# Attention of a hybrid trunk: probabilities stationary against both parts of v, a fixed softmax order, the residual loaded again, and GpSimd work moved

## The chip, the cores and the metric

The kernel runs on one core of one Trainium2 chip. The metric is the device time of one execution in microseconds, as the median of several runs. The profile shows one more execution of the same program: TensorE (PE, with its weight loads as PEld), VectorE (DVE), ScalarE (ACT), GpSimd (POOL) and SyncE's DMA queue (SP).

## The reference

One sequence of 512 tokens and 1024 features goes through four residual layers: attention, MLP, S5 state-space layer, MLP. The change lies in the first layer and in what is made for the third beside the first MLP. The attention is:

```python
c_q, c_kv, k_r, q_b, k_b, v_b = jnp.split(h @ w_in, IN_SPLITS, axis=-1)
q = (rms_norm(c_q, g_cq) @ w_uq).reshape(B, S, MLA_HEADS, MLA_QK).transpose(0, 2, 1, 3)
kv = (rms_norm(c_kv, g_ckv) @ w_ukv).reshape(B, S, MLA_HEADS, MLA_NOPE + MLA_V).transpose(0, 2, 1, 3)
...
s = jnp.einsum('bhqd,bhkd->bhqk', q[:, :, lo:hi], k[:, :, :hi]).astype(jnp.float32)
mask = jnp.arange(hi)[None, :] <= jnp.arange(lo, hi)[:, None]
p = jax.nn.softmax(jnp.where(mask, s, -jnp.inf), axis=-1).astype(v.dtype)
outs.append(jnp.einsum('bhqk,bhkd->bhqd', p, v[:, :, :hi]))
...
return o @ w_o
```

There are 8 latent heads (key width 96) and 8 MoBA heads (key width 64), values 64 wide. With 512 tokens in blocks of 256, a MoBA query's chosen past block and its own block are all the keys before it, so both kinds are causal attention over 512 tokens. The layer's output is added to x. The S5 layer is a convolution whose tables come from its parameters alone.

## The kernel before, in words

Every large product is made in three matmuls: an operand is split into a rounded part and the rest ("hi" and "lo", of type fp32r), and hi·hi, hi·lo and lo·hi are added in PSUM (`mm3`, L116 to L120). A weight tile is loaded by SP's queue (L109 or L155), its hi part is a copy on ACT (L112, L171), its lo part a subtraction on DVE (L113) or on the engine that is passed in (L172).

**Front** (`split_x`, L329 to L341, and `proj`, L343 to L366). For each of 8 slices of x: hi part on ACT (L331), lo part on DVE (L332), the square on POOL for even slices (L334, L340) and on ACT for odd ones (L338), the running sum of squares on POOL (L341); then the slice of w_in is split (L358 ACT, L359 DVE), and 12 matmuls follow (L362 to L364).

**The attention loop** (L622 to L644) takes 16 heads (8, 9, then 0 to 7, then 10 to 15) of 4 query blocks each, 64 steps (h, b), in a pipeline: in step i, block i+1 is transposed (stage c), block i+2 gets its exponentials (stage b), block i+3 its scores (stage a), and block i its product with v (stage d). Stage a makes the scores by three matmuls and a mask matmul (L522 to L525) and the row maxima on DVE (L527). Stage b is the exponential on ACT with its row sum (L535), the reciprocal on DVE (L536), and the scaling of the row by it (L537: ACT for odd b, DVE for even). Stage c transposes each 128 keys on PE (L545), copies the hi part on ACT (L548) and subtracts the lo part on DVE (L549). Stage d holds 64 columns of v stationary and streams 128 queries, three matmuls for each 128 keys (L564 to L566); after a head's last block its 64 x 512 output is split (L570 ACT, L571 DVE). The order of instructions on an engine is a scheduler's, which may move them past one another.

Between the steps stands filler work for PE, taken from lists (`segs`, L615) at an even rate: projections of MoBA pairs 1 to 3 from step -3 to 37, and the first half of the output projection w_o from step 42 to 62. The latter (`w_o1_items`) splits its weights with `gp`, POOL, as the engine of the lo part (L587, L172), and adds the residual in two steps, hi part and product on DVE (L599), lo part on POOL (L600). The tile xT of the residual, a buffer with one copy, held x and then the values v of heads 0 to 7.

**The S5 tables** (generator L890 to L994) are made during the first MLP. `pump` (L1387) advances the generator after each group of matmuls, and `behind` keeps a step's instructions after DVE's and POOL's last ones. Unit u of 16 makes W and its companion on POOL (L899, L901) and CP on DVE (L905, L907), rotates on POOL (L936 to L938) with a copy on ACT (L939) and a store (L940), places B (L946, L947), splits tables (L915 to L923), and multiplies them on PE (L955 to L957). W, CP and RT have two buffers each.

Of the kernel before, what the change touches and what calls it, by code (L numbers as in the profile page):

```python
# [45 lines left out]
class Trunk:  # L46
# [130 lines left out]
    def attention(self, xt, w_in, gmix, g_cq, w_uq, g_ckv, w_ukv, gains, rope, w_o, mlp):  # L177
# [24 lines left out]
        def moba_pair_items(p):  # L202
# [20 lines left out]
            def start():  # L223
                d["qk"] = mo.tile([P, NT, 4, 64], F32, name="qk", bufs=3)
                d["vh"] = mo.tile([P, NT, 2, 64], F32R, name="vh", bufs=3)
                d["vl"] = mo.tile([P, NT, 2, 64], F32R, name="vl", bufs=3)
                d["ss"] = mo.tile([P, NT, 4], F32, name="mss")
                d["r"] = mo.tile([P, NT, 4], F32, name="mr")
                self.pairs[p] = d["qk"], d["vh"], d["vl"]

            def unit(t, q):
# [9 lines left out]
                if q == 3:  # L241
# [3 lines left out]
                    vt = d["vh"][:, t].rearrange("p a d -> p (a d)")  # L245
                    sc.activation(vt, ps[:, 256:], AF.Copy, scale=rt)
                    ve.scalar_tensor_tensor(d["vl"][:, t].rearrange("p a d -> p (a d)"), ps[:, 256:], rt,
                                            f32(d["vh"])[:, t].rearrange("p a d -> p (a d)"),
                                            op0=OP.mult, op1=OP.subtract)
# [46 lines left out]
        with tc.tile_pool(name="att_e", bufs=1) as ep:  # L296
# [16 lines left out]
            for h in range(2):  # L313
# [10 lines left out]
            a = mo.tile([P, 1024], F32R, name="qk", bufs=3)  # L324
            cTs = [[a[:, j * 384:(j + 1) * 384].rearrange("p (c q) -> p c q", c=3) for j in range(2)],
                   [mo.tile([P, NT, 2, 64], F32R, name=v, bufs=3).rearrange("p t a d -> p (t a d)")
                    [:, :384].rearrange("p (c q) -> p c q", c=3) for v in ("vh", "vl")]]

            def split_x(k):  # L329
# [156 lines left out]
        O1 = [[op.tile([P, S], F32R, name=f"o1{2 * p + a}") for a in range(2)] for p in range(4)]  # L486
        O2 = [[op.tile([P, S], F32R, name=f"o2{a}") for a in "hl"]]
# [26 lines left out]
        st = {}  # L514

        def stage_a(h, b):
# [5 lines left out]
            pe.matmul(s[:, :n], q[0][rows, bs], k[0][rows, :n], start=True, stop=False)  # L522
# [3 lines left out]
            m = hd.tile([P, 4], F32, name="st", bufs=6)  # L526
            ve.reduce_max(m[:, 0:1], s[:, :n], axis=AX.X, negate=True)  # L527
            st[h, b] = dict(s=s, m=m)

        def stage_b(h, b):  # L530
# [4 lines left out]
            sc.activation(p[:, :n], d["s"][:, :n], AF.Exp, bias=m[:, 0:1], accum_out=m[:, 1:2])  # L535
            ve.reciprocal(m[:, 2:3], m[:, 1:2])  # L536
            sc.activation(p[:, :n], p[:, :n], AF.Copy, scale=m[:, 2:3]) if b % 2 else ve.tensor_scalar(p[:, :n], p[:, :n], m[:, 2:3], None, op0=OP.mult)  # L537

        def stage_c(h, b):
# [3 lines left out]
            for j in range(b + 1):  # L543
                js = slice(j * P, (j + 1) * P)
                pe.transpose(pt[:, js], d["p"][:, js], self.ident)  # L545
            ph = d["ph"] = hd.tile([P, 512], F32R, name="ph")
            pl = d["pl"] = hd.tile([P, 512], F32R, name="pl")
            sc.copy(ph[:, :n], pt[:, :n])  # L548
            ve.tensor_sub(pl[:, :n], pt[:, :n], f32(ph)[:, :n])  # L549

        def stage_d(h, b):
# [3 lines left out]
            po = st[h]  # L555
            if h < 8:
                v = vm_hi[:, :, h], vm_lo[:, :, h]
            else:
                _, vh, vl = self.pairs[(h - 8) // 2]
                v = vh[:, :, h % 2], vl[:, :, h % 2]  # L560
            bs = slice(b * P, (b + 1) * P)
            for j in range(b + 1):
                js = slice(j * P, (j + 1) * P)
                pe.matmul(po[:64, bs], v[0][:, j], d["ph"][:, js], start=j == 0, stop=False)  # L564
                pe.matmul(po[:64, bs], v[0][:, j], d["pl"][:, js], start=False, stop=False)
                pe.matmul(po[:64, bs], v[1][:, j], d["ph"][:, js], start=False, stop=j == b)  # L566
# [960 lines left out]
```

## Time and profile before

| | us |
|---|---|
| time, median of 3 runs | 1217.16 (1216.47 to 1218.07) |
| time of the profiled execution | 1217.28 |
| span from the first to the last instruction in it | 1215.5 |
| PE busy | 1155.7 (95%), 6296 matmuls |
| DVE busy | 788.6 (65%) |
| ACT busy | 501.2 (41%) |
| POOL busy | 257.9 (21%) |
| mean granted TensorE clock | 0.973 of full speed |

PE is busy nearly everywhere, so the stretches in which it is not, or in which its clock is below full speed, are what one reads first. The page cuts the span into 40 equal slices of 30.4 us (counted here from 0). PE's busy share is 7 tenths in slice 0, the front; 8 tenths in slice 2, where the attention loop begins, and in slices 14 and 16, from about 425 us; and 7 to 8 tenths in slices 22 to 24, the S5 layer itself, whose code the change leaves. The clock is at 7 to 8 tenths in slices 6 and 7, about 182 to 243 us, in slice 15, and in slices 22 to 24. The front lies at 0 to 32 us, the attention loop at about 62 to 276, the first MLP with the S5 tables at about 300 to 560.

### The profile page before, as it was taken

How to read it: one execution, taken by the hardware profiler on the slowest of the kernel's cores; microseconds unless marked ns; L12 is line 12 of the kernel's file. 1: busy time of each engine (PE TensorE's matmuls, PEld its weight loads, DVE VectorE, ACT ScalarE, POOL GpSimd, SP SyncE). 2: the span in 40 equal slices, each digit the busy share in tenths (PEclk: the TensorE clock that was granted, in tenths of full speed). 3: DMA queues.
4: the chain of work that ended last, by engine and by line, in shares of the span. 5: the costliest groups of instructions: out<-in, count | busy, mean ns of one | idle time of the engine just before them, and what ended most of it. 6: DMA issues, size and time to landing. Idle time of an engine off the chain costs nothing.

```text
span 1215.5 us, 16433 instructions
## 1 busy us (share of the span) xinstructions
PE 1155.7 (95%) x6296; PEld 963.5 (79%) x6296; DVE 788.6 (65%) x1381; ACT 501.2 (41%) x928; POOL 257.9 (21%) x260
## 2 busy tenths in 40 slices
PE   7989999999999989899999788999999999999998
PEld 6978997777888867788888576878788888888887
DVE  8887766668679979998855576553454444444444
ACT  5857775545331333352352265343341331322221
POOL 5461022224000588652300031111000000000000
PEclk9999997899999998999999788999999999999999
DMA  7302201114422357777769789522322332322421
GB/s 223 103 3 53 70 2 70 36 36 154 140 79 95 104 189 237 223 217 216 227 212 339 229 284 323 178 94 80 104 104 70 104 105 70 113 95 70 139 87 52
DMA packets 123758, 161.94 MB, mean 133 GB/s; under 512 B 15648, under 2 KB 72352, under 8 KB 120992
## 3 DMA queue, kind: packets, MB, share of 16 engines
q1 hardware_dynamic: 123680, 160.90, 40.8%
q8 instruction: 49, 0.80, 0.3%
q14 instruction: 29, 0.24, 0.1%
HBM read 133.75 MB, written 35.52 MB: 139 GB/s over the span
## 4 chain that ended last, share of the span: by engine, by line
PE 75%; DVE 9%; DMA 5%; POOL 4%; ACT 4%; issue 2%; SPq 1%; ACTq 0%; DVEq 0%; POOLq 0%
PE mm L118 14%; PE mm L120 14%; PE mm L119 14%; PE s L120 5%; PE s L118 5%; PE s L119 5%; DVE wlo L113 2%; PE pt L545 1%; PE mm L238 1%; PE mm L239 1%; PE mm L240 1%; DMA dX<-xT 1%; PE s L522 1%; PE pt L493 1%; POOL RT L938 1%
## 5 line engine op out<-in xcount | busy, mean ns | idle before, releaser
L112 ACT CAST whi<-wraw 128x1024 fp32r<-128x1024 f32 x132 | 131.8, 1048 | 229.7 <-PE mm L119 136.3
L113 DVE TENSOR_TENSOR wlo<-wraw,whi 128x1024 fp32r<-128x1024 f32 x132 | 168.7, 1307 | 77.4 <-ACT whi L112 77.3
L118 PE MATMUL mm<-ahi,whi 128*128 128x512 f32 (+1 forms) x352 | 135.8, 388 | 2.4 <-ACT ahi L1417 2.4
L119 PE MATMUL mm<-alo,whi 128*128 128x512 f32 (+1 forms) x352 | 136.3, 389 | 1.3 <-DVE alo L1418 1.3
L118 PE MATMUL mm<-xhi,whi 128*128 128x512 f32 x344 | 135.7, 394 | 0.0
L119 PE MATMUL mm<-xlo,whi 128*128 128x512 f32 x344 | 134.9, 392 | 0.0
L120 PE MATMUL mm<-xhi,wlo 128*128 128x512 f32 x344 | 133.5, 394 | 1.0 <-DVE wlo L113 1.0
L120 PE MATMUL mm<-ahi,wlo 128*128 128x512 f32 (+1 forms) x352 | 134.0, 386 | 0.0
L118 PEld LDWEIGHTS mm<-ahi,whi 128*128 128x128 f32 x352 | 66.6, 189 | 16.4 <-ACT ahi L1417 3.3
L119 PEld LDWEIGHTS mm<-alo,whi 128*128 128x128 f32 x352 | 66.6, 189 | 15.6 <-DVE alo L1418 2.5
L120 PEld LDWEIGHTS mm<-xhi,wlo 128*128 128x128 f32 x344 | 64.5, 188 | 16.2 <-DVE wlo L113 1.4
L118 PEld LDWEIGHTS mm<-xhi,whi 128*128 128x128 f32 x344 | 64.5, 188 | 14.9 <-issue 0.5
L120 PEld LDWEIGHTS mm<-ahi,wlo 128*128 128x128 f32 x352 | 66.1, 188 | 12.8
L119 PEld LDWEIGHTS mm<-xlo,whi 128*128 128x128 f32 x344 | 64.6, 188 | 14.7 <-issue 0.2
L1442 DVE TENSOR_TENSOR mm<-mm,bcast 128x512 f32<-128x512 f32 (+1 forms) x44 | 29.9, 683 | 67.5 <-PE mm L120 67.4
L118 PE MATMUL s<-ahi,whi 128*128 128x512 f32 x168 | 65.8, 392 | 3.0 <-ACT whi L112 3.0
L118 PE MATMUL s<-xhi,whi 128*128 128x512 f32 x168 | 66.2, 394 | 0.0
L119 PE MATMUL s<-xlo,whi 128*128 128x512 f32 x168 | 66.0, 393 | 0.0
L120 PE MATMUL s<-xhi,wlo 128*128 128x512 f32 x168 | 65.6, 393 | 0.0
L119 PE MATMUL s<-alo,whi 128*128 128x512 f32 x168 | 65.6, 391 | 0.0
L120 PE MATMUL s<-ahi,wlo 128*128 128x512 f32 x168 | 65.2, 390 | 0.0
L899 POOL TENSOR_TENSOR W<-PW,B 128x512 f32<-128x512 f32 x16 | 24.8, 1548 | 166.9 <-DVE B L888 121.4
(485 smaller groups left out, 2863.0 us busy)
## 6 DMA issues: line engine op xcount, KB each, us to landing
wraw<-in_w_ff SPq DMA_DIRECT2D x64, 1024.0 KB
dC<-wC SPq DMA_DIRECT2D x16, 512.0 KB
dB<-wB SPq DMA_DIRECT2D x16, 512.0 KB
wraw<-in_w_glu SPq DMA_DIRECT2D x16, 512.0 KB
tT<-dT SPq DMA_DIRECT2D x7, 1024.0 KB
wraw<-in_w_in SPq DMA_DIRECT2D x24, 256.0 KB
tB<-dB SPq DMA_DIRECT2D x6, 1024.0 KB
tC<-dC SPq DMA_DIRECT2D x6, 1024.0 KB
```

Of the source, the lines that this page charges most:

```text
L112: nc.scalar.copy(hi[:, s, :n], raw[:, s, :n])
L113: nc.vector.tensor_sub(lo[:, s, :n], raw[:, s, :n], f32(hi)[:, s, :n])
L118: te.matmul(ps, whi, xhi, start=start, stop=False)
L119: te.matmul(ps, whi, xlo, start=False, stop=False)
L120: self.last = te.matmul(ps, wlo, xhi, start=False, stop=stop).ins
L238: pe.matmul(ps, hhi[:, k, tsl[t]], wh[:, k4, :384], start=k == 0, stop=False)
L239: pe.matmul(ps, hhi[:, k, tsl[t]], wl[:, k4, :384], start=False, stop=False)
L240: pe.matmul(ps, hlo[:, k, tsl[t]], wh[:, k4, :384], start=False, stop=k == 7)
L493: pe.transpose(pt[:w, t], blocks[t], self.ident)
L522: pe.matmul(s[:, :n], q[0][rows, bs], k[0][rows, :n], start=True, stop=False)
L899: gp.tensor_mul(dst, pw[a][:, :, 1:9, None].to_broadcast(bc), B[a][:, gs][:, :, None, :].to_broadcast(bc))
L1442: ve.tensor_mul(ps[:, s], ps[:, s], self.Rb[:, s])
```

## The change

- Front: all eight squares are made on ACT, the running sum on DVE; POOL has none of it.
- The two parts of v lie in one tile, beside each other for each block of keys. In stage d the transposed probabilities (hi part, then lo part) are stationary, 128 columns of them, and 128 columns stream: v's hi part and v's lo part. That is two matmuls for 128 keys in place of three. The output has tokens on partitions.
- The probabilities aren't scaled: row sums are gathered per head, and at the head's end DVE takes 4 reciprocals in one instruction, ACT copies the lo half, DVE adds the hi half and scales. After each pair of heads 4 transposes bring the result back to features on partitions, where it is split, 128 x 512 at a time.
- The first scores matmul, the first transpose, the exponentials, the maxima and the two parts are held in program order, and the order of a step is written anew.
- x, laid out as xT is, is loaded again into xT once head 7 is done; a single DVE addition takes the place of L599 and L600. The lo part of the w_o weights in the loop is made on DVE.
- Filler of the MoBA pairs reaches to step 42.
- In the S5 tables, unit u's rotations are issued before unit u+1 is made.

```diff
@@ split_x
                 if k == 0:
-                    gp.tensor_mul(acc, x0[:, k], x0[:, k])
+                    sc.activation(acc, x0[:, k], AF.Square)
                 else:
                     sq = hd.tile([P, S], F32, name="p", bufs=3)
-                    if k % 2:
-                        sc.activation(sq, x0[:, k], AF.Square)
-                    else:
-                        gp.tensor_mul(sq, x0[:, k], x0[:, k])
-                    gp.tensor_add(acc, acc, sq)
+                    sc.activation(sq, x0[:, k], AF.Square)
+                    ve.tensor_add(acc, acc, sq)
@@ stages a, b and c
-            ve.reduce_max(m[:, 0:1], s[:, :n], axis=AX.X, negate=True)
+        def maxima(h, b):
+            d = st[h, b]
+            keep(ve.reduce_max(d["m"][:, 0:1], d["s"][:, :(b + 1) * P], axis=AX.X, negate=True))
...
-            sc.activation(p[:, :n], d["s"][:, :n], AF.Exp, bias=m[:, 0:1], accum_out=m[:, 1:2])
-            ve.reciprocal(m[:, 2:3], m[:, 1:2])
-            sc.activation(p[:, :n], p[:, :n], AF.Copy, scale=m[:, 2:3]) if b % 2 else ve.tensor_scalar(p[:, :n], p[:, :n], m[:, 2:3], None, op0=OP.mult)
+            keep(sc.activation(p[:, :n], d["s"][:, :n], AF.Exp, bias=m, accum_out=sums[h][:, b:b + 1]))
...
-            sc.copy(ph[:, :n], pt[:, :n])
-            ve.tensor_sub(pl[:, :n], pt[:, :n], f32(ph)[:, :n])
+            keep(sc.copy(ph[:, :n], pt[:, :n]))
+            keep(ve.tensor_sub(pl[:, :n], pt[:, :n], f32(ph)[:, :n]))
@@ stage_d
-            for j in range(b + 1):
-                js = slice(j * P, (j + 1) * P)
-                pe.matmul(po[:64, bs], v[0][:, j], d["ph"][:, js], start=j == 0, stop=False)
-                pe.matmul(po[:64, bs], v[0][:, j], d["pl"][:, js], start=False, stop=False)
-                pe.matmul(po[:64, bs], v[1][:, j], d["ph"][:, js], start=False, stop=j == b)
+            for n, ph in enumerate((d["ph"], d["pl"])):
+                for j in range(b + 1):
+                    pe.matmul(po[:, b], ph[:, j * P:(j + 1) * P], v[:, :, j], start=n + j == 0, stop=n == 1 and j == b)
             if b == 3:
-                sc.copy(o[0][orow], po[:64])
-                ve.tensor_sub(o[1][orow], po[:64], f32(o[0])[orow])
+                r = sums.pop(h)
+                ve.reciprocal(r, r)
...
+                sc.copy(t, po[:, :, 1])
+                ve.tensor_add(t, po[:, :, 0], t)
+                ve.tensor_mul(ot[:, :, h % 2], t, r[:, :, None].to_broadcast([P, NT, 64]))
+                if h % 2:
+                    pt = self.ptp.tile([P, NT, P], F32, name="pt")
+                    for t in range(NT):
+                        pe.transpose(pt[:, t], ot[:, t].rearrange("p a d -> p (a d)"), self.ident)
...
+                    sc.copy(o[0], pf)
+                    ve.tensor_sub(o[1], pf, f32(o[0]))
                 if h == 7:
                     self.xT = self.xpool.tile([P, KT, S], F32, name="xT")
+                    for k in range(0, KT, 4):
+                        nc.sync.dma_start(self.xT[:, k:k + 4],
+                                          xl[k * P:(k + 4) * P].rearrange("(k p) s -> p k s", p=P))
@@ w_o1_items and segs
-                self.split_rows(*d[mh], d["raw"], 512, slice(2 * h, 2 * h + 2), gp)
+                self.split_rows(*d[mh], d["raw"], 512, slice(2 * h, 2 * h + 2))
...
-                    ve.tensor_add(xm, in_chunks(f32(hhi)[:, m]), in_chunks(d["ps"]))
-                    gp.tensor_add(xm, xm, in_chunks(f32(hlo)[:, m]))
+                    ve.tensor_add(xm, xm, in_chunks(d["ps"]))
...
-        segs = [(-3, 37, moba_items([1, 2, 3])), (42, 62, wo1)]
+        segs = [(-3, 42, moba_items([1, 2, 3])), (42, 62, wo1)]
@@ the loop's step
-            stage_c(i + 1), stage_b(i + 2), stage_a(i + 3) with its maxima, prep, filler, stage_d(i)
+            stage_b(i + 2), stage_c(i + 1), stage_a(i + 3), parts(i + 1), maxima(i + 3), prep, filler, stage_d(i)
@@ S5 tables
-                now, made = made, make(u + 1) if u < 15 else None
+                now = made
                 rotations(u // 2, u % 2)
+                made = make(u + 1) if u < 15 else None
```

The hunk of the loop's step is shortened to the order of its calls.

On PE, in the loop beside the MoBA projections (L238 to L240), the kernel before has this, where the three matmuls of the product with v (L564 to L566) have the stationary v as `xT`:

```order
L523 MATMUL s<-klo,qhi 128x256
L524 MATMUL s<-khi,qlo 128x256
L525 LDWEIGHTS identb
L525 MATMUL s<-maskb,identb 128x128
L564 MATMUL mm<-ph,xT 64x128
L565 MATMUL mm<-pl,xT 64x128
L566 MATMUL mm<-ph,xT 64x128
L564 MATMUL mm<-ph,xT 64x128
L565 MATMUL mm<-pl,xT 64x128
L566 MATMUL mm<-ph,xT 64x128
L545 MATMUL pt<-ident,p 128x128 x4
L564 MATMUL mm<-ph,xT 64x128
```

After the change a step reads, here beside the w_o product (L118 to L120), with the probabilities stationary:

```order
L545 MATMUL pt<-ident,p 128x128 x3
L516 MATMUL s<-khi,qhi 128x128
L517 MATMUL s<-klo,qhi 128x128
L518 MATMUL s<-khi,qlo 128x128
L519 LDWEIGHTS identb
L519 MATMUL s<-maskb,identb 128x128
L120 MATMUL mm<-o_2303,wlo 128x512
L118 MATMUL mm<-o_2586,whi 128x512
L119 MATMUL mm<-o_2587,whi 128x512
L120 MATMUL mm<-o_2586,wlo 128x512
L569 MATMUL mm<-v,ph 128x128 x2
L569 MATMUL mm<-v,pl 128x128 x2
```

Transposes, scores, filler and the product with v stand in that order in every step, and no scores or transposes stand inside a product any more.

On ACT, in the first MLP, the kernel before has these rows around the split of two weight tiles (L112); RT are the rotations, wB and wC the split tables, the numbers are buffers:

```order
L939 ACTIVATE RT_5217<-RT_5217 128x8x32
L939 ACTIVATE RT_5326<-RT_5326 128x8x32
L939 ACTIVATE RT_5452<-RT_5452 128x8x32
L946 CAST bzh_3957<-B2_3942 128x4x16
L959 COPY kt_4999<-pt_4986 64x112
L915 CAST wC_5149<-CP_4897 128x576
L922 CAST wB_5015<-pt_5010 128x512
L962 CAST Ks_5002<-kt_4999 64x128
L939 ACTIVATE RT_5561<-RT_5561 128x8x32
L939 ACTIVATE RT_5728<-RT_5728 128x8x32
L112 CAST whi_5165<-wraw_5164 128x1024 x2
L112 CAST whi_5173<-wraw_5172 128x1024 x2
```

After the change the same place has (L968 is the rotations' copy, L944 and L951 are the tables'):

```order
L968 ACTIVATE RT_4905<-RT_4905 128x8x32
L1447 CAST ahi_4768<-fp_4764 128x512
L991 CAST Ks_4679<-kt_4676 64x128
L975 CAST bzh_3786<-B2_3771 128x4x16
L988 COPY kt_4828<-pt_4815 64x112
L944 CAST wC_4978<-CP_4733 128x576
L951 CAST wB_4844<-pt_4839 128x512
L991 CAST Ks_4831<-kt_4828 64x128
L112 CAST whi_4994<-wraw_4993 128x1024 x2
L112 CAST whi_5002<-wraw_5001 128x1024 x2
```

Five copies of rotations that stood ahead of the weight split in these rows no longer stand there; one is left, well ahead of it.

## Rows read from the trace of the kernel before

**Rows 1.** Chain that ended last, the whole span, shares by engine:
```profile
PE 75%; DVE 9%; DMA 5%; POOL 4%; ACT 4%; issue 2%; SPq 1%; ACTq 0%; DVEq 0%; POOLq 0%
```

**Rows 2.** Busy windows: length, engines' busy us (instructions), PEclk, DMA share, GB/s; PE, PEld, DVE, ACT, POOL:
```profile
20.00:40.00 20.00, 19.61 (x105) 19.36 (x106) 16.19 (x39) 10.61 (x31) 7.54 (x26) 0.91 0.46 120
...
62.00:100.00 38.00, 35.05 (x221) 29.98 (x221) 30.84 (x88) 21.79 (x54) 20.95 (x31) 1.00 0.00 1
...
180.00:220.00 40.00, 36.37 (x214) 28.03 (x211) 25.11 (x65) 20.44 (x52) 12.64 (x10) 0.79 0.15 53
220.00:276.00 56.00, 53.49 (x351) 42.13 (x351) 36.04 (x75) 28.71 (x69) 11.12 (x6) 0.94 0.12 39
...
420.00:440.00 20.00, 16.57 (x78) 12.21 (x77) 19.66 (x19) 8.60 (x17) 20.00 (x15) 1.00 0.70 230
440.00:460.00 20.00, 14.41 (x74) 11.15 (x73) 12.35 (x22) 6.43 (x15) 14.21 (x19) 0.93 0.54 172
460.00:480.00 20.00, 20.00 (x98) 16.34 (x97) 19.97 (x22) 5.67 (x12) 17.99 (x15) 0.89 0.75 240
480.00:500.00 20.00, 16.25 (x82) 13.00 (x81) 19.23 (x20) 7.42 (x15) 19.84 (x17) 1.00 0.67 212
```

**Rows 3.** Timeline of DVE in the front: start, us, instructions:
```profile
7.12 0.69 DVE L332 TENSOR_TENSOR hlo<-xT,hhi 128x512 fp32r<-128x512 f32 x1
...
9.42 3.23 DVE L332 TENSOR_TENSOR hlo<-xT,hhi 128x512 fp32r<-128x512 f32 x2
```

**Rows 4.** Waits, 0 to 32 us: total us, times, longest:
```profile
PE mm L364 <- DVE wlo L359: 2.3, 1, 2.3
```

**Rows 5.** Groups by line, 62 to 276 us: busy us, mean ns, idle before:
```profile
L537 ACT ACTIVATE p<-p,st 128x256 f32<-128x256 f32 (+1 forms) x32 | 19.7, 616 | 7.4 <-DVE st L536 7.3
...
L537 DVE TENSOR_SCALAR p<-p,st 128x128 f32<-128x128 f32 (+1 forms) x32 | 13.7, 429 | 0.4
...
L536 DVE RECIPROCAL st<-st 128x1 f32<-128x1 f32 x64 | 9.6, 155 | 2.0 <-ACT p L535 1.4
L172 POOL TENSOR_TENSOR wlo<-wraw,whi 128x1024 fp32r<-128x1024 f32 x4 | 9.4, 2368 | 7.8 <-ACT whi L171 7.8
```

**Rows 6.** The same by shape, 62 to 276 us:
```profile
L549 DVE TENSOR_TENSOR pl<-pt,ph 128x512 fp32r<-128x512 f32 x16 | 11.0, 686 | 5.6 <-ACT ph L548 5.6
...
L549 DVE TENSOR_TENSOR pl<-pt,ph 128x256 fp32r<-128x256 f32 x16 | 6.7, 417 | 8.0 <-ACT ph L548 8.0
```

**Rows 7.** Timeline of PE in the loop: start, us, instructions, idle before:
```profile
139.99 0.22 PE L565 MATMUL mm<-pl,xT 128*64 128x128 f32 x1
140.05 0.22 PE L566 MATMUL mm<-ph,xT 128*64 128x128 f32 x1
...
178.91 0.31 PE L523 MATMUL s<-klo,qhi 96*128 96x128 f32 x1
179.05 0.28 PE L524 MATMUL s<-khi,qlo 96*128 96x128 f32 x1
...
179.97 0.62 PE L545 MATMUL pt<-ident,p 128*128 128x128 f32 x4
181.67 0.27 PE L564 MATMUL mm<-ph,xT 128*64 128x128 f32 x1 [1.08 <-ACT ph L548]
```

**Rows 8.** Timeline of SP's queue at the loop's second half:
```profile
182.00 5.60 SPq L109 DMA_DIRECT2D wraw<-in_w_o  x2
```

**Rows 9.** Waits, 400 to 530 us: total us, times, longest:
```profile
ACT RT L939 <- POOL RT L938: 50.3, 16, 5.2
...
PE s L118 <- ACT whi L112: 3.0, 1, 3.0
```

**Rows 10.** Timeline of ACT in the first MLP:
```profile
457.91 0.42 ACT L939 ACTIVATE RT<-RT 128x256 f32<-128x256 f32 x1 [1.67 <-POOL RT L938]
458.23 3.87 ACT L112 CAST whi<-wraw 128x1024 fp32r<-128x1024 f32 x4
```

More of the change, by code (lines that the diff above doesn't have):

```diff
@@ L175, in load_wg, with attention @@
         return self.split_w(self.raw_w(srcs, kts), kts, sum(s.shape[1] for s in srcs), eng=eng)
-    def attention(self, xt, w_in, gmix, g_cq, w_uq, g_ckv, w_ukv, gains, rope, w_o, mlp):
+    def attention(self, xt, xl, w_in, gmix, g_cq, w_uq, g_ckv, w_ukv, gains, rope, w_o, mlp):
         nc, tc = self.nc, self.tc
@@ L244, in unit @@
                     sc.activation(qkt, ps[:, :256], AF.Copy, scale=rt)
[L245 to L249, printed above, removed]
+                    vh, vl = (d["v"][:, a, t].rearrange("p a d -> p (a d)") for a in range(2))
+                    sc.activation(vh, ps[:, 256:], AF.Copy, scale=rt)
+                    ve.scalar_tensor_tensor(vl, ps[:, 256:], rt, f32(vh), op0=OP.mult, op1=OP.subtract)
                     sq = mo.tile([P, 4, 64], F32, name="msq")
@@ L322, in attention @@
             W = {}
[L324 to L327, printed above, removed]
+            cTs = []
+            for n in ("qk", "v"):
+                a = mo.tile([P, 1024], F32R, name=n, bufs=3)
+                cTs.append([a[:, j * 384:(j + 1) * 384].rearrange("p (c q) -> p c q", c=3) for j in range(2)])
             def split_x(k):
@@ L485, in attention @@
                     qk(t - 1)
-        O1 = [[op.tile([P, S], F32R, name=f"o1{2 * p + a}") for a in range(2)] for p in range(4)]
-        O2 = [[op.tile([P, S], F32R, name=f"o2{a}") for a in "hl"]]
+        O1, O2 = [], []
         def qk_tiles(name, blocks, w, gain):
@@ L512, in prep @@
                     P, (gq_mo, gk_mo)[a])
-        st = {}
+        keep = tc.keep_in_program_order
+        st, sums, otok, o2p = {}, {}, [None], []
         def stage_a(h, b):
@@ L521, in stage_a @@
             s = self.psp.tile([P, 512], F32, name="s")
-            pe.matmul(s[:, :n], q[0][rows, bs], k[0][rows, :n], start=True, stop=False)
+            keep(pe.matmul(s[:, :n], q[0][rows, bs], k[0][rows, :n], start=True, stop=False))
             pe.matmul(s[:, :n], q[0][rows, bs], k[1][rows, :n], start=False, stop=False)
@@ L525, in stage_a @@
             pe.matmul(s[:, bs], self.identb, self.mask, start=False, stop=True)
[L526 to L527 removed]
+            m = hd.tile([P, 1], F32, name="st", bufs=6)
+            if b == 0:
+                sums[h] = hd.tile([P, NT], F32, name="sum", bufs=3)
             st[h, b] = dict(s=s, m=m)
+        def maxima(h, b):
+            d = st[h, b]
+            keep(ve.reduce_max(d["m"][:, 0:1], d["s"][:, :(b + 1) * P], axis=AX.X, negate=True))
         def stage_b(h, b):
@@ L622, in attention @@
         for i in range(-3, n):
+            if 0 <= i + 2 < n:
+                stage_b(*seq[i + 2])
             if 0 <= i + 1 < n:
                 stage_c(*seq[i + 1])
+            if i + 3 < n:
+                stage_a(*seq[i + 3])
             if 0 <= i + 2 < n:
-                stage_b(*seq[i + 2])
+                scale(*seq[i + 2])
+            if 0 <= i + 1 < n:
+                parts(*seq[i + 1])
             if i + 3 < n:
                 h, b = seq[i + 3]
-                stage_a(h, b)
+                maxima(h, b)
                 nx = heads.index(h) + 1
@@ L1470, in trunk @@
         T.s5_dram(dp)
-        xT, mlp = T.attention(i["xt"], i["w_in"][0], gmix0, gcq, i["w_uq"][0], gckv, i["w_ukv"][0], gains,
+        xT, mlp = T.attention(i["xt"], i["xl"], i["w_in"][0], gmix0, gcq, i["w_uq"][0], gckv, i["w_ukv"][0], gains,
                               i["rope"], i["w_o"][0],
@@ L1503, in layout @@
     out = {n: a[n] for n in ("mix_norm_g", "w_in", "w_uq", "w_ukv", "w_o", "w_glu", "w_ff1", "w_ff2")}
-    out.update(xt=a["x"][0].T, gains=gains, s5p=s5p, s5b=s5b, s5c=s5c, s5d=s5d, rope=rope_table())
+    xt = a["x"][0].T
+    out.update(xt=xt, xl=xt.reshape(D, S // 8, 8).transpose(0, 2, 1).reshape(D, S), gains=gains, s5p=s5p, s5b=s5b, s5c=s5c, s5d=s5d, rope=rope_table())
     return {n: np.ascontiguousarray(v) for n, v in out.items()}
```

39 lines of the change are left out of this document (26 added, 13 removed).

## The prediction

> **What bounds the kernel now.** I read the chain that ended last first, then the busy windows, then timelines and waits where a window was short of full. The chain is PE for 75% [rows 1]: time can be won only where PE stands idle, runs at a low clock, or gets less to do. The windows [rows 2] show where that is, in the stretches that the change touches. In the front, 20 to 40 us, the granted clock is 0.91. In the attention loop PE is idle for 2.95 us in 62 to 100, 3.63 us in 180 to 220 and 2.51 us in 220 to 276, some 9.1 us; and at 0.79 and 0.94 of full clock the last two lose some 8.4 + 3.4 = 11.8 us more. So about 21 us of the loop's 214 aren't PE's work. In the S5 tables, PE is idle for 3.43, 5.59 and 3.75 us in 420 to 440, 440 to 460 and 480 to 500, 12.8 us in all, and 0.93 and 0.89 of clock in 440 to 480 cost 1.4 + 2.2 = 3.6 us. After the first MLP the instructions stand in the same order as before, so I give the rest nothing.
>
> The sum is made against the profiled execution, 1217.28 us (span 1215.5), which lies 0.1 us above the median of the three runs. About 0.2% (2.4 us) is what a measurement of this kernel tells from no change.
>
> **The front.** Eight squares go to ACT and seven sums to DVE, none stay on POOL. A DVE subtraction with two inputs in SBUF took 0.69 us at 7.12, but two of them took 3.23 us at 9.42, when POOL was at its squares and sums [rows 3]: 1.6 us each. Were all eight x subtractions and the similar weight subtractions (L359, a fifth shorter) at 0.65 to 0.69 us, and seven sums of 0.69 us added, DVE would have 16 x 0.67 + 7 x 0.69 = 15.5 us of work against some 21 us that it spends now, from 4 to 25 us. PE waits 2.3 us for one such lo part [rows 4] and then runs at half clock for a while: the 0.91 over 20 us is 1.8 us. ACT gets four more squares; it has 10.6 us of work in 20 us [rows 2]. Gain: 2.3 + 1.8 = 4.1 us. Taken: **-4 us**; bounds -5.5 (all that DVE gains) and -1 (ACT becomes late in its place).
>
> **The product with v.** Before, 16 heads x 10 key blocks x 3 = 480 matmuls; their starts are 0.06 us apart where nothing is late [rows 7], 28.8 us in all. Now 320, each with 128 stationary columns and 128 moving ones. The nearest rows: four transposes of 128 x 128 take 0.62 us, the last of them about 0.29 itself, so 0.11 us apart; two scores matmuls with 128 stationary columns and 128 moving start 0.14 us apart [rows 7]. That gives 35.2 to 44.8 us. The transposes are nearest (one behind another, all 128 rows), so I take 0.11. The 32 transposes of the results add 3.5 us. Sum: 35.2 + 3.5 - 28.8 = **+10 us** of PE work; at 0.14, +19.5. So fewer matmuls are no saving: both parts of v ride on one load, but the load is twice as wide.
>
> What rows show is 0.11 us. The Trainium skill (TensorE: Matmul & The Clock Gate, Back-to-back issue gap) gives a measured pace of about 81 ns for a stream of load and matmul at 128 columns. By that the term would be 25.9 + 3.5 - 28.8 = +0.6 us, an estimate from that page, in place of +10. No stream of exactly this shape is in the trace; the transposes there are slower than the page's pace.
>
> **What the loop gets back.** The scaling goes: 19.7 us on ACT, 13.7 on DVE, and 9.6 of reciprocals [rows 5]. These lie on the way from scores to transposes, not on PE's own time. DVE gets per head a reciprocal (0.16), an addition and a scaling of 256 elements (0.42 each), in place of a split of 64 x 512, and per pair a split of 0.69 [rows 6]: 16 x 1.0 + 8 x 0.69 = 21.5 us, against 23.3 + 16 x 0.69 = 34.3 removed. The weights' lo part moves from POOL, where four took 2.37 us each [rows 5], to DVE, at about twice 0.69 us: +5.5. DVE ends with some 7 us less, ACT with some 20 less, both out of about 150 and 130. More telling is the order. Each step now makes exponentials, parts and maxima one whole step, 3.3 us, before PE wants them. A wait such as 1.08 us for L548 at 181.67, behind the w_o load's split on ACT and DVE [rows 7, 8], has that much cover. And MoBA filler reaches to step 42, so steps 37 to 42 aren't bare. I take three quarters of the 21 us as won: **-16 us**. With the +10 the loop gives **-6 us**. Bounds: +10 if nothing is won and -11 if everything is; at 0.14 us a matmul, up to +19.5.
>
> The residual: 2 MB on SP's queue behind the w_o loads, which need 5.6 us for two issues [rows 8]. The release is head 7's last product, at about 42/67 of the loop, near 197 us; 1 MB loads land within 5 us there, so xT would be whole near 207. The first addition stands some 6 us of PE work behind the release. DVE may be held for 0 to 3 us, and then the next lo part is late; the step of cover hides most of that. Taken: 0, bound +3. L600 on POOL isn't waited for: nothing.
>
> **The S5 tables.** RT's ACT copies wait 50.3 us in total for POOL [rows 9], and they stand ahead of the next weight split in ACT's queue. At 457.91 such a copy begins after 1.67 us of idling for POOL, the weight split L112 follows at 458.23 [rows 10], and PE waits 3.0 us for it [rows 9]. With the rotations issued one per unit, one copy instead of five lies in that stretch. What remains: DVE and POOL are both full for 20 us at 420, and nearly so at 460 and 480 [rows 2], and the same amounts of W, CP and RT must be made there. So I expect somewhat over half of the 12.8 + 3.6 = 16.4 us: **-9 us**. Bounds: 0, if the waits only move, and -16.
>
> Sum: 1217.3 - 4 - 6 - 9 = **1198 us**.
>
> **The rivals.**
> *A: the tables don't gain.* DVE and POOL slow each other whenever both work on SBUF, as [rows 3] show, so the pair is the bound of the stage, not the place of a copy; full windows on both [rows 2] speak for it, 3.0 us for a single split behind a POOL wait [rows 9] against it. Then 1217.3 - 4 - 6 = 1207 us. The Trainium skill (SBUF — State Buffer, SBUF: two separate sides) says that the two engines' shared ports are an exclusive lock, under which the one that comes second blocks fully; the 0.69 against 1.6 us agrees with that.
>
> *B: slower, by the stationary load.* If the probabilities' loads set 0.14 us or more for each of the 320 matmuls, as the two scores matmuls do [rows 7], PE's work grows by 19.5 us, all of it on the path, since PE is the path. If the loop's waits then stay (because they come from the clock and the transitions rather than from late operands), the loop costs +19.5, and 1217.3 - 4 + 19.5 - 9 = 1224 us. It decides from the point where growth exceeds what the loop wins plus 13: with nothing won, from (13 + 28.8 - 3.5) / 320 = 0.12 us; with half won, 0.15 us. Against it: the transposes at 0.11. The Trainium skill (TensorE: Matmul & The Clock Gate, LDWEIGHTS (loading the stationary operand)) says that a load's time goes by its columns, at 1.2 per ns: 107 ns for these, 53 for v's; by that the pace is 0.107, near what I took.
>
> *C: the waits all go.* Loop -11, tables -16, front -5: 1185 us. For it: an order with a full step of cover; against it, DVE and POOL full at 420.
>
> *D: no change,* 1215 to 1220 us: the loop's gain and the +10 cancel and the tables only shift. That needs three mild disappointments.
>
> **How the numbers follow.** The forecast's case (1190 to 1204) gets 0.49, A (1204 to 1213) 0.22, C 0.14 (1180 to 1190), D 0.06, B 0.09. The range is to hold 8 in 10: it takes in the forecast, A, and the half of C that is nearer, down to 1185; the top is 1214, where D and B begin. Faster by over 0.2%: 0.49 + 0.22 + 0.14 = 0.85; D gives 0.06, B 0.09.
>
> **What would show it.** Right: in the front, DVE's L332 all near 0.69 us and no half clock after 20 us. In the loop, the product's matmuls 0.11 us apart, no PE wait over 1 us between 180 and 205, and a clock near 1.0 there. In the tables, PE over 18 of 20 us busy in each of the windows from 420 to 500. Wrong: matmuls of 0.14 us; DVE waiting for the residual's DMA near 200 us with PE idle behind it; PE still at 14 to 16 of 20 us beside full DVE and POOL.

## The result and the profile after

The changed kernel took 1250.28 us (median of 4 runs, 1247.9 to 1252.49) against 1217.62 us before (1216.47 to 1218.54): a ratio of 1.0268, 95% interval 1.0244 to 1.0292. It is 33 us slower, where 1198 us, 19 us faster, was forecast, and it lies outside the range of 1185 to 1214. The profiled execution took 1251.68 us, span 1250.0, clock 0.958.

The chain of the kernel after is still PE's, with a larger share than in [rows 1]:

```profile
PE 77%; DVE 9%; ACT 4%; DMA 3%; POOL 3%; issue 2%; SPq 1%; ACTq 0%; DVEq 0%; POOLq 0%
```

The busy windows of the kernel after, columns as in [rows 2]; the first scores of the attention loop start at 68.7 us (67.5 before), and its last product with v at 307.2 (274.0 before):

```profile
20.00:40.00 20.00, 20.00 (x117) 19.46 (x116) 14.54 (x49) 14.91 (x47) 5.59 (x26) 1.00 0.49 126
...
62.00:100.00 38.00, 32.78 (x160) 27.16 (x160) 25.27 (x63) 13.55 (x37) 16.57 (x23) 0.82 0.00 1
...
140.00:180.00 40.00, 34.90 (x226) 31.87 (x225) 26.43 (x68) 22.81 (x62) 4.01 (x7) 0.91 0.16 54
180.00:220.00 40.00, 35.61 (x223) 31.68 (x222) 25.46 (x61) 20.43 (x52) 4.34 (x7) 0.90 0.17 59
220.00:260.00 40.00, 38.21 (x199) 30.07 (x199) 22.44 (x42) 16.99 (x45) 0.00 (x0) 0.84 0.21 74
260.00:300.00 40.00, 38.18 (x169) 29.76 (x169) 19.17 (x36) 13.64 (x36) 0.00 (x0) 0.76 0.08 27
...
440.00:460.00 20.00, 19.30 (x91) 15.73 (x90) 19.66 (x20) 6.73 (x11) 15.90 (x11) 1.00 0.30 101
460.00:480.00 20.00, 16.45 (x85) 12.20 (x84) 18.43 (x21) 7.71 (x16) 16.54 (x14) 1.00 0.63 217
480.00:500.00 20.00, 20.00 (x103) 16.70 (x102) 19.19 (x31) 7.60 (x14) 6.50 (x6) 1.00 0.76 236
```

The front did as forecast (clock 1.00 in 20 to 40 us). The loop is where the time went: its last product comes 33.2 us later, nearly all of the 34.5 us by which the span grew. DVE and ACT have less to do in it than before, and yet PE is idle for 4 to 5 us in each of three windows, and its clock is at 0.76 to 0.91 from 140 us on. Less work on the side engines came with more waiting for them. The S5 tables begin some 33 us later, so their windows don't match those of before one to one.

What the steps of the loop look like is plain from 13 rows. ACT (columns: start, us, operation, idle before it and what ended it):

```profile
193.68 0.60 ACT L534 ACTIVATE p<-s,st 128x384 f32<-128x384 f32 x1
...
194.25 0.39 ACT L555 CAST ph<-pt 128x256 fp32r<-128x256 f32 x1
195.81 0.69 ACT L534 ACTIVATE p<-s,st 128x512 f32<-128x512 f32 x1 [1.18 <-DVE st L527]
...
197.78 0.37 ACT L534 ACTIVATE p<-s,st 128x128 f32<-128x128 f32 x1 [0.82 <-DVE st L527]
```

DVE, the same time:

```profile
194.77 0.41 DVE L556 TENSOR_TENSOR pl<-pt,ph 128x256 fp32r<-128x256 f32 x1
195.10 0.68 DVE L527 TENSOR_REDUCE st<-s 128x1 f32<-128x512 f32 x1
...
196.99 0.56 DVE L556 TENSOR_TENSOR pl<-pt,ph 128x384 fp32r<-128x384 f32 x1 [0.19 <-ACT ph L555]
197.47 0.28 DVE L527 TENSOR_REDUCE st<-s 128x1 f32<-128x128 f32 x1
```

PE, the same time, and a product with 4 stationary loads:

```profile
193.75 0.23 PE L519 MATMUL s<-maskb,identb 128*128 128x128 bf16 x1
194.67 0.52 PE L545 MATMUL pt<-ident,p 128*128 128x128 f32 x3 [0.69 <-ACT ph L555]
...
195.61 0.39 PE L569 MATMUL mm<-xT,pl 128*128 128x128 f32 x2
196.65 0.66 PE L545 MATMUL pt<-ident,p 128*128 128x128 f32 x4 [0.65 <-ACT p L534]
...
198.77 0.66 PE L569 MATMUL mm<-xT,ph 128*128 128x128 f32 x4
```

The scores of the 512-wide block were complete about 194.0 (mask matmul at 193.75). Its maxima (L527) start only at 195.10, since the lo part of an older block (L556) stands ahead of them on DVE; that one waited for its hi part (L555, 194.25 on ACT), which stands behind the exponentials of a third block (L534, 193.68). The next exponentials wait for those maxima until 195.81. So exponentials, hi part, lo part, maxima, exponentials run one after another across two engines: a ring, and ACT and DVE take turns. I call it the ring below. PE meets it at its transposes, 0.65 us late, with nothing else before them in its order that is ready. Only the first transpose and the first scores matmul of a step are held, and so, against what was said ahead of the prediction, products are still cut in two: the four stationary loads at 198.77 are the hi part alone, and a transpose (199.50) and scores (199.58) follow before the lo part.

### The profile page after: what moved, and what is told of

Read it like the earlier page. It is cut to its first block, busy times and chain, and to the rows that moved or that the text cites. A ratio compares the mean times of both kernels' runs of the same rounds, so it can differ in the third digit from the quotient of the medians.

```text
span 1250.0 us, 16137 instructions
## 1 busy us (share of the span) xinstructions
PE 1183.4 (95%) x6168; PEld 988.6 (79%) x6168; DVE 776.1 (62%) x1336; ACT 485.0 (39%) x908; POOL 218.2 (17%) x237
## 4 chain that ended last, share of the span: by engine, by line
PE 77%; DVE 9%; ACT 4%; DMA 3%; POOL 3%; issue 2%; SPq 1%; ACTq 0%; DVEq 0%; POOLq 0%
PE mm L118 14%; PE mm L120 14%; PE mm L119 14%; PE s L118 6%; PE s L119 6%; PE s L120 5%; PE mm L569 2%; DVE wlo L113 2%; PE pt L545 1%; PE mm L237 1%; PE mm L238 1%; PE mm L239 1%; PE s L516 1%; DMA dX<-xT 1%; POOL t L928 1%
## 5 line engine op out<-in xcount | busy, mean ns | idle before, releaser
L112 ACT CAST whi<-wraw 128x1024 fp32r<-128x1024 f32 x132 | 131.7, 1048 | 226.1 <-PE mm L119 128.4
L118 PE MATMUL mm<-ahi,whi 128*128 128x512 f32 (+1 forms) x352 | 135.5, 386 | 1.9 <-ACT ahi L1447 1.1
L118 PE MATMUL mm<-xhi,whi 128*128 128x512 f32 x344 | 136.2, 396 | 0.0
L120 PE MATMUL mm<-xhi,wlo 128*128 128x512 f32 x344 | 134.4, 396 | 0.3 <-DVE wlo L113 0.3
L120 PE MATMUL mm<-ahi,wlo 128*128 128x512 f32 (+1 forms) x352 | 134.1, 386 | 0.0
L118 PEld LDWEIGHTS mm<-ahi,whi 128*128 128x128 f32 x352 | 66.1, 188 | 15.9 <-ACT ahi L1447 1.9
L120 PEld LDWEIGHTS mm<-xhi,wlo 128*128 128x128 f32 x344 | 64.9, 189 | 15.5 <-DVE wlo L113 0.7
L118 PEld LDWEIGHTS mm<-xhi,whi 128*128 128x128 f32 x344 | 64.9, 189 | 14.9 <-issue 0.5
L120 PEld LDWEIGHTS mm<-ahi,wlo 128*128 128x128 f32 x352 | 66.1, 188 | 12.8
L118 PE MATMUL s<-xhi,whi 128*128 128x512 f32 x168 | 66.4, 395 | 0.0
L120 PE MATMUL s<-xhi,wlo 128*128 128x512 f32 x168 | 65.7, 393 | 0.0
L118 PE MATMUL s<-ahi,whi 128*128 128x512 f32 x168 | 65.6, 390 | 0.0
L120 PE MATMUL s<-ahi,wlo 128*128 128x512 f32 x168 | 65.3, 390 | 0.0
```

What stands on the lines that cost most here:

```text
L112: nc.scalar.copy(hi[:, s, :n], raw[:, s, :n])
L118: te.matmul(ps, whi, xhi, start=start, stop=False)
L120: self.last = te.matmul(ps, wlo, xhi, start=False, stop=stop).ins
```

## The experiments

Each ratio is against the kernel before, run on the same chip; the kernel before took 1215.2 to 1218.0 us (medians) on the chips used, so a difference between two experiments is good to a few us. The rivals of the first set: theory 1, the ring; theory 2, the wide stationary side; theory 3, filler in lumps.

**Maxima ahead of the parts.**

```diff
-            if 0 <= i + 1 < n:
-                parts(*seq[i + 1])
             if i + 3 < n:
-                h, b = seq[i + 3]
-                maxima(h, b)
+                maxima(*seq[i + 3])
+            if 0 <= i + 1 < n:
+                parts(*seq[i + 1])
```

> The change with one swap: in each step the maxima of block i+3 come ahead of the two parts of block i+1 on DVE. Theory 1 (the held order makes a ring: exponentials, hi part on ACT, lo part on DVE, maxima on DVE, next exponentials, each behind the last, so that ACT and DVE take turns, about 2.1 us of work and 0.6 us of handing over in each of 64 steps): the maxima no longer stand behind the lo part, the waits of TensorE for exponentials in the loop go, the clock stays up, and the time falls by 15 to 30 us, to 1220 to 1235. Theory 2 (128 stationary columns make TensorE's own work the longer part): no more than 3 us, 1247 or above. Theory 3 (what is not held, the filler, clumps, and steps without filler are bare): TensorE's order is the same as in the change, so at most 8 us, 1242 or above.

Measured: 1243.9 us, ratio 1.0219 (1.0195 to 1.0243), 6 us less than the change. The sign is theory 1's, the size isn't: the time lies in the range that theory 3 gave. ACT's wait for the maxima fell, from the first row (the change) to the second (this kernel), in the loop; columns: total us, times, longest:

```profile
ACT p L534 <- DVE st L527: 37.9, 36, 1.8
```
```profile
ACT p L534 <- DVE st L527: 17.8, 23, 1.8
```

So half of the ring's waiting was worth only 6 us: more than the ring is at work.

**Nothing held.** `keep` returns its instruction unchanged.

```diff
-        keep = tc.keep_in_program_order
+        keep = lambda ins: ins
```

> The change with nothing held in program order; everything else stays. Theories 1 and 3: the scheduler places maxima, parts and filler freely as before the change, and the time falls to 1215 to 1230. Theory 2: the wide stationary operand costs as much in any order, 1245 or above.

Measured: 1226.45 us, 1.0066 (1.004 to 1.0092). Holding costs 24 us, the largest part. The rest, +9 us against before, remains with nothing held, and theory 2 has a share in that.

**S5 order as before.**

```diff
-                now = made
+                now, made = made, make(u + 1) if u < 15 else None
                 rotations(u // 2, u % 2)
-                made = make(u + 1) if u < 15 else None
```

> The change with the order of the S5 tables as before (unit u+1 made ahead of unit u's rotations). If the milestones in the two traces tell it (35 us behind at 450 us, 24 at 530, 31 at 690, 34 from 890 on), the new order gains 10 and gives them back by the end of the S5 layer: 1250 within 3 us. If the new order is worth the 9 us that were forecast: 1256 to 1262.

Measured: 1255.43 us, 1.031 (1.0286 to 1.0334): 5 us more than the change. Both expectations miss: the new order is worth about 5 us, neither 0 nor 9.

**The front alone**, on the kernel before: its `split_x` as in the change.

> The kernel before with only the front changed: squares on ScalarE, sums on VectorE. If the gain of the front (the projection ends 4 us earlier in the change) is kept to the end: 1213, 3 to 5 us less than before. Rival: it is given back before the first scores, which in the change start 0.9 us later than before: 1216 to 1219.

Measured: 1217.93 us, 1.0015 (0.9998 to 1.0033): no difference. The rival holds. Windows of the kernel before and of this one, where the loop begins:

```profile
62.00:80.00 18.00, 15.05 (x77) 11.92 (x78) 14.07 (x39) 8.93 (x23) 13.70 (x23) 1.00 0.00 0
```
```profile
62.00:80.00 18.00, 16.14 (x69) 12.88 (x68) 15.87 (x48) 8.99 (x25) 10.62 (x16) 0.75 0.01 1
```

Here the clock is at 0.75 with the front changed and 1.00 without: 18 x 0.25 = 4.5 us, as much as the front had won. But that is not shown to be the reason: the first scores start at 68.0 us here, against 67.5 before, so the front's lead doesn't reach the loop, and the clock is still at 1.00 from 62 to 71 us. And the kernel with the S5 order alone (below), whose front and loop are those of before, has a low clock there too:

```profile
62.00:80.00 18.00, 15.97 (x64) 12.22 (x63) 13.50 (x34) 9.18 (x21) 12.86 (x22) 0.77 0.00 0
```

The swap explains a quarter of what holding costs, so the next set asks whose holding it is. Theory 4: PE's order.

**Only TensorE held**, then **only ACT and DVE held**.

```diff
-            keep(sc.activation(p[:, :n], d["s"][:, :n], AF.Exp, bias=m, accum_out=sums[h][:, b:b + 1]))
+            sc.activation(p[:, :n], d["s"][:, :n], AF.Exp, bias=m, accum_out=sums[h][:, b:b + 1])
...
```

The first drops `keep` from exponentials, parts and maxima; the second from the scores and transposes instead.

> The change with only TensorE's first scores matmul and first transpose held, ACT and DVE free. If the ring on ACT and DVE were the cost of holding (theory 1): as with nothing held, 1224 to 1230. If it is TensorE's order (theory 4: each transpose stands ahead of the next scores and of the product, so TensorE stops at it whenever the exponentials are late, with scores and products ready behind it): 1240 to 1250. The swap of the maxima gave 6 of 24 us, so I lean to theory 4.

Measured: 1234.52 us, 1.0155 (1.0115 to 1.0195), between the two ranges.

> The change with only exponentials, the two parts and the maxima held, TensorE free. Theory 1: 1240 to 1250. Theory 4: 1224 to 1232.

Measured: 1256.49 us, 1.0322 (1.0284 to 1.0361). That lies above both ranges, and the leaning to theory 4 was wrong: the sides are the costlier to hold, 30 us over nothing held, against 8 for PE. With the sides held, holding PE too even helps by 6.

**Filler held as well**, with maxima ahead of the parts:

```diff
-                    pe.matmul(ps, hhi[:, k, tsl[t]], wh[:, k4, :384], start=k == 0, stop=False)
+                    i = pe.matmul(ps, hhi[:, k, tsl[t]], wh[:, k4, :384], start=k == 0, stop=False)
+                    if p and k == 2 * q:
+                        tc.keep_in_program_order(i)
```

> All held, maxima ahead of the parts, and also the first matmul of each quarter unit of the MoBA projections held, so that 6 filler matmuls stand in each step of the loop's first 42 in place of 24 in one step and none in three. Theory 3 (bare steps are what makes the held order wait): the first 42 steps run without waits at full clock, 15 us less than with the maxima swapped alone: 1224 to 1232. Otherwise within 4 us of 1244.

Measured: 1239.29 us, 1.0186 (1.0153 to 1.0219): 5 us less than 1243.9, a third of what theory 3 asked, and the two intervals overlap.

**Old product, nothing held.** Stages b and d as before the change, on the kernel with nothing held.

```diff
+            ve.reciprocal(m[:, 2:3], m[:, 1:2])
+            sc.activation(p[:, :n], p[:, :n], AF.Copy, scale=m[:, 2:3]) if b % 2 else ve.tensor_scalar(p[:, :n], p[:, :n], m[:, 2:3], None, op0=OP.mult)
...
-                    pe.matmul(po[:, b], ph[:, j * P:(j + 1) * P], v[:, :, j], start=n + j == 0, stop=n == 1 and j == b)
+                pe.matmul(po[:64, bs], v[0][:, j], d["ph"][:, js], start=j == 0, stop=False)
+                pe.matmul(po[:64, bs], v[0][:, j], d["pl"][:, js], start=False, stop=False)
+                pe.matmul(po[:64, bs], v[1][:, j], d["ph"][:, js], start=False, stop=j == b)
```

> The change with nothing held, and with scaled probabilities, v stationary and three matmuls for 128 keys as before the change (parts of v in one tile, w_o split on DVE, residual loaded again, S5 order and front stay). If the wide stationary side costs TensorE the 10 us that the forecast gave it (theory 2): 1226 - 10 = 1216, 1212 to 1218. If the product costs nothing net: 1224 to 1228. If the unscaled softmax relieves ACT and DVE in a way that matters: above 1230.

Measured: 1212.65 us, 0.9968 (0.9947 to 0.9988). So the product with its unscaled softmax and transposes costs 12 us by the ratios and 14 by the medians, and what is left of the change (front, residual, w_o on DVE, filler to step 42, S5 order) wins 4 to 5. By the traces, only half of the product's cost lies in the loop: it ends at 281.2 us with nothing held and at 273.9 here, 7.3 us of the 16.9 between these two profiled executions. The rest comes behind the loop, in stages whose code is the same in both, and why is open.

**Sides held, maxima ahead.** The swap of the first experiment on the kernel with only ACT and DVE held.

> The kernel with only ACT's and DVE's steps held, and the maxima of block i+3 ahead of the parts of block i+1. Theory 1 (the ring exponentials, hi part, lo part, maxima, next exponentials is what holding the sides costs): 1230 to 1242, 15 us or more less than the 1256 with the maxima behind. Theory 5 (any held order on ACT and DVE costs this much, since other work of theirs, projections' copies and head ends, then stands in the way): 1250 or above.

Measured: 1244.57 us, 1.0234 (1.0213 to 1.0256): 12 us less than 1256.49. ACT's waits for maxima in the loop, with the maxima behind the parts, then ahead of them:

```profile
ACT p L534 <- DVE st L527: 40.5, 44, 2.0
```
```profile
ACT p L534 <- DVE st L527: 15.9, 22, 2.0
```

That is 3 us short of theory 1's gain and far from theory 5: the ring is shown, with a price of some 12 us here and 6 when PE is held too. With nothing held the same wait is 7.5 us in all; some 18 us of the holding remains without the ring.

**S5 order alone**, the change's order on the kernel before.

> The kernel before with only the order of the S5 tables changed. In the change, undoing it cost 5 us. If it is worth the same by itself: 1212 to 1214. If it is worth the 9 us that were forecast: 1208 to 1210. If its gain there came from the shifted start: 1217.

Measured: 1213.1 us, 0.9963 (0.9946 to 0.9981). It keeps its 4 to 5 us by itself.

**Old product, spread filler.** On the kernel with the old product, PE's scores, transposes and filler held as above.

> The variant with the old product and nothing held (1212.7), and now TensorE's first scores matmul, first transpose and the first matmul of each MoBA quarter unit held, so that filler is spread at 6 matmuls a step. If spread filler covers the softmax better than the scheduler's lumps of 24: 1205 to 1210, better than both kernels. If holding TensorE costs its 8 us again and the spreading gives back 5: 1213 to 1217.

Measured: 1229.05 us, 1.0082 (1.005 to 1.0114), 16 us more than without holding. Both ranges were missed, and the six executions go from 1219.6 to 1232.1. Spread filler is no gain here; the run holds TensorE and spreads the filler at once, so it can't tell which of the two costs.

**Where the rest of the holding lies.** Heads 12 to 15, in windows from the first product of head 12 to the last of head 15: the change, nothing held, and only TensorE held:

```profile
243.50:307.20 63.70, 60.31 (x276) 47.87 (x274) 29.57 (x54) 21.99 (x55) 0.00 (x0) 0.76 0.10 34
```
```profile
232.40:281.20 48.80, 46.58 (x272) 37.03 (x270) 28.84 (x53) 20.86 (x53) 0.00 (x0) 1.00 0.14 44
```
```profile
232.90:295.60 62.70, 57.64 (x276) 45.95 (x275) 29.21 (x53) 22.61 (x55) 0.00 (x0) 0.81 0.10 34
```

The same work takes 63.7 us in the change and 48.8 with nothing held: 15 of the 26 us by which the loop ends later (307.2 against 281.2). The clock is at 0.76 against 1.00, and 63.7 x 0.24 = 15 us is as much as the whole difference. With only the sides held it is much the same (the traces of these two are of the slowest of their four executions):

```profile
255.80:318.90 63.10, 57.97 (x272) 45.94 (x271) 29.03 (x53) 21.42 (x54) 0.00 (x0) 0.78 0.11 34
```

The other 11 us lie in the heads before, from the first product to head 12: 167.5 us in the change, 162.0 with the maxima ahead, 156.0 with the filler held as well, 156.7 with nothing held. So there the ring is worth some 5 us and the lumps of filler some 6, by one trace each, and theory 3 has its share: in these heads a held order with both mended is as fast as a free one. Two traces of the same loop can lie 4 us apart (it ends at 274.0 before and at 269.8 with the S5 order alone).

The rows at the first long stop of heads 12 to 15 in the change, on PE, ACT and DVE:

```profile
248.11 0.23 PE L519 MATMUL s<-maskb,identb 128*128 128x128 bf16 x1
249.75 0.69 PE L569 MATMUL mm<-v,ph 128*128 128x128 f32 x2 [1.41 <-ACT ph L555]
...
246.38 2.00 ACT L112 CAST whi<-wraw 128x1024 fp32r<-128x1024 f32 x2 [2.34 <-PE mm L119]
248.29 0.57 ACT L592 CAST o2h<-pt 128x512 fp32r<-128x512 f32 x1
248.76 0.58 ACT L534 ACTIVATE p<-s,st 128x384 f32<-128x384 f32 x1
...
249.33 0.37 ACT L555 CAST ph<-pt 128x256 fp32r<-128x256 f32 x1
...
247.60 2.34 DVE L113 TENSOR_TENSOR wlo<-wraw,whi 128x1024 fp32r<-128x1024 f32 x2
```

and the windows after it:

```profile
250.00:255.00 5.00, 4.84 (x20) 3.65 (x21) 2.84 (x7) 2.19 (x6) 0.00 (x0) 0.50 0.66 210
255.00:260.00 5.00, 5.00 (x23) 4.34 (x23) 1.97 (x5) 1.41 (x4) 0.00 (x0) 0.50 0.02 5
```

With nothing held, the same place on PE and ACT:

```profile
237.15 0.38 PE L545 MATMUL pt<-ident,p 128*128 128x128 f32 x2
238.26 0.44 PE L569 MATMUL mm<-v,ph 128*128 128x128 f32 x2 [0.73 <-ACT ph L555]
...
235.28 2.00 ACT L112 CAST whi<-wraw 128x1024 fp32r<-128x1024 f32 x2 [1.59 <-PE mm L119]
237.35 0.58 ACT L592 CAST o2h<-pt 128x512 fp32r<-128x512 f32 x1
237.83 0.38 ACT L555 CAST ph<-pt 128x256 fp32r<-128x256 f32 x1
```

A weight split of 2.0 us stands on ACT in both. With nothing held, the hi part follows it at once and PE has two blocks' scores to do before; it stops for 0.73 us, and the window's clock stays at 1.00. Held, the exponentials come first, PE has one block's scores, it stops for 1.41 us, and the granted clock is 0.50 of full speed, the 1.2 GHz level, from 250 to 260 us. The stop itself is small; at half clock PE loses about 5 us in these 10.

That order on ACT isn't the only way to the same loss. With only TensorE held, ACT's hi part also follows at once, and PE stops for 0.83 us there; a longer stop comes at the next transposes, which wait for a lo part on DVE (L594) behind the weight split:

```profile
238.57 0.44 PE L570 MATMUL mm<-v,ph 128*128 128x128 f32 x2 [0.83 <-ACT ph L556]
240.67 0.52 PE L546 MATMUL pt<-ident,p 128*128 128x128 f32 x3 [1.66 <-DVE o2l L594]
```

With nothing held PE has two blocks' scores to do ahead of the first stop, in the change and with TensorE held it has one. That this is what the held orders have in common is argued from these rows; no run tests it. Nor did a run hold the order and put the lo part of the w_o weights back on POOL, as in the kernel before.

The last run frees the order there alone. Theory 6 is this.

```diff
-        keep = tc.keep_in_program_order
+        on = [True]
+        keep = lambda ins: tc.keep_in_program_order(ins) if on[0] else ins
...
         for i in range(-3, n):
+            on[0] = i < 42
```

> The change with everything held as in it for steps -3 to 41, and nothing held from step 42 on, where the first half of w_o is the filler (heads 12 to 15 and a little of head 11). Theory 6: of the 24 us that holding costs, some 15 arise in the last four heads, which take 64 us in the change and 49 with nothing held, since weight splits of 2.0 us on ACT and 2.3 us on DVE stand ahead of held instructions there, TensorE stops for 1.4 to 1.6 us behind them, and its clock is at half for about 12 us after each stop: 1232 to 1238, and the last four heads in 47 to 52 us. If the cost is of holding anywhere alike (19 of 67 steps freed): 1242 to 1245.

Measured: 1235.42 us, 1.0195 (1.0131 to 1.0258), by medians 15 us less than the change, by the ratios some 9. Heads 12 to 15 in this kernel:

```profile
241.40:290.20 48.80, 46.17 (x271) 36.80 (x270) 29.01 (x53) 20.95 (x53) 0.00 (x0) 1.00 0.14 44
```

48.8 us at full clock, as with nothing held. Theory 6 is shown for the place, and for the size in this trace. The total is less sure: one of the four executions took 1246.48 us, and the interval, wider than in the other runs, touches the change's (1.0244 to 1.0292). That the clock, rather than the order as such, carries most of it rests on the rows above: no run kept the order and the clock both.

## Why the prediction was wrong

By medians: front 0, S5 order and the small parts -5, product +14, holding +24, together +33. They add up because each is the step to the next kernel of a row (before; old product, nothing held; nothing held; the change). The traces show them by stage. The loop ends at 274.0, 273.9, 281.2 and 307.2 us in these four, as the windows from head 12 on show for the first two:

```profile
224.80:274.00 49.20, 47.35 (x304) 37.55 (x303) 31.52 (x64) 25.11 (x58) 9.58 (x5) 0.93 0.14 44
```
```profile
226.40:273.90 47.50, 46.34 (x304) 36.31 (x302) 29.48 (x64) 24.85 (x58) 0.00 (x0) 0.96 0.14 45
```

So the loop, forecast at -6 us, measured +33: some +7 from the product and +26 from holding. Part by part, as the prediction had them:

- **The front, -4.** The mechanism was right: DVE's subtractions all near 0.69 us, the clock 1.00 after 20 us, the projection 4 us earlier. The mis-sized step is that a gain at 27 us would last to the end: the projection ends 4.8 us earlier with the front alone (26.5 against 31.3 us), and the first scores start 0.5 us later. Measured: 0. What the first scores wait for instead is open.
- **The product, +10.** Right in sign and in pitch: one of these matmuls takes 0.28 us (median), so the two of 0.39 us at 195.61 start 0.11 us apart and the four of 0.66 at 198.77 0.13, against 0.11 taken and 0.14 as a bound. Measured as a whole: +12 to +14, with the unscaled softmax's relief in it, and +7 of that in the loop. The Trainium skill's pace of about 81 ns (TensorE: Matmul & The Clock Gate, Back-to-back issue gap) doesn't hold for this stream; the page's load time by columns in LDWEIGHTS (loading the stationary operand), 107 ns for 128 columns, is near it.
- **What the loop gets back, -16.** This is the step that failed. I read "one whole step, 3.3 us, before PE wants them" off the order of the calls and took it for cover, without following each held engine's queue round: who stands behind whom on ACT and DVE. The maxima of block i+3 stand behind the lo part of block i+1, and the exponentials ahead of the hi part, and so the cover is spent in the queue. Then the weight splits, which the scheduler may put anywhere, stood ahead of held instructions that couldn't be changed round. In place of -16 the runs show +24 (+26 in the loop's traces): some 6 of it the ring, some 5 the lumps of filler, 15 in the last four heads, at the lower clock. One row was misread as well: the wait of 1.08 us at 181.67 stood behind the weight split's hi part on ACT alone, for its lo part was on POOL [rows 5]. The longest wait there, 1.80 us at 186.51 for DVE's L549, came just before the clock fell (0.50 from 190 to 200 us); it stood behind a scaling of 128 x 128 that took 2.43 us on DVE while POOL's L172 ran.
- **The small parts at 0.** The residual: SP issued it at 217 us, and in the waits DVE's L623 waited for TensorE alone, 7.5 us in 6 waits, never for that DMA. Zero was right for the parts together: what is left without product and holding takes 1212.65 us, the S5 order alone 1213.1.
- **The S5 tables, -9.** Mechanism right, size off: -4 to -5 at the end, and once more a gain that wasn't kept. In the kernel with the S5 order alone, 440 to 460 and 460 to 480 are full at clock 1.00, but 420 to 440 is as short as before, and it stays short later:

```profile
420.00:440.00 20.00, 16.50 (x77) 12.12 (x76) 18.75 (x21) 7.74 (x16) 17.50 (x15) 1.00 0.69 236
440.00:460.00 20.00, 20.00 (x111) 16.75 (x110) 18.98 (x29) 7.60 (x14) 5.52 (x5) 1.00 0.72 224
460.00:480.00 20.00, 20.00 (x111) 16.66 (x110) 17.66 (x21) 5.47 (x11) 19.94 (x16) 1.00 0.54 171
...
500.00:560.00 60.00, 57.62 (x290) 47.99 (x289) 52.80 (x69) 25.71 (x48) 30.94 (x24) 0.97 0.72 222
```

In 500 to 560 before, PE was busy for 59.30 us at clock 1.00. The rotations that no longer run ahead in 410 to 460 are done there, so a part of the gain came back as waits. More comes back in the S5 layer, whose code is the same. Its first matmuls on PE, before and with the S5 order alone:

```profile
L1106 PE MATMUL pt<-sacc,halves x16: 219/219/245, 679.5 to 679.7; 128*32 128x64 f32 x16
```
```profile
L1107 PE MATMUL pt<-sacc,halves x16: 219/219/245, 669.9 to 670.1; 128*32 128x64 f32 x16
```

The layer starts 9.6 us earlier, 4.2 of them from the loop, so the tables' stage won 5.4 where 9 was forecast; but the span is only 4.0 us shorter (1211.5 against 1215.5). In the change it is alike: the loop ends 33.2 us later, the layer starts 28.7 us later (708.2), the span is 34.5 us longer. Why the layer takes longer behind the new order is open.

Rival B had the sign and half of the mechanism (the wider load), and put its point of decision, 0.12 us a matmul with nothing won in the loop, where the pitch turned out to be; what it didn't have is that the loop could lose rather than merely not win. No rival held an order that makes waits. That was the missing case.

What beats both kernels: the S5 order alone, 1213.1 us, or all of the change but its product and its holding, 1212.65 us; the two aren't told apart. Both are by 0.3 to 0.4%, with intervals that end below 1.

## What to carry to other kernels

An order held by hand has to be followed along every engine's queue, not along the steps: write down, for each held instruction, the one ahead of it on its engine and that one's last input, and see whether the chain comes back to the next step's first instruction. Take the work that isn't held into account too, since a 2 us split may land ahead of a held instruction. Price two narrow loads against one wide load by the pace of stationary loads, not by the number of matmuls.

## What the runs showed of the hardware

In the change, a stop of TensorE of 1.41 us stood at the head of more than 10 us at half the granted clock, while one of 0.73 us in the same place with nothing held left the clock at full. At full clock, neighbouring matmuls of the product with v started 0.11 to 0.13 us apart with 128 stationary columns, and 0.06 us apart with 64 [rows 7], 128 columns moving in both. A gain in one stage can be given back in a later one whose code is the same: 4 us of the front before the first scores, and, with the S5 order alone, 5.6 us between the start of the S5 layer and the end.
